# A third buffer for the gate rows and an earlier load of the output weights in the mixing stage of a hybrid decoder layer

## The chip, the cores and the metric

The kernel runs on one core of a Trainium2 chip. The metric is the device time of one execution in microseconds, as the median of several runs. The core has five engines with a queue each, worked off in order: TensorE (PE; its weight loads are shown apart as PEld), VectorE (DVE), ScalarE (ACT), GpSimd (POOL) and SyncE (SP). Here SP computes nothing, it only issues transfers between HBM and on-chip memory; POOL computes and issues some transfers too.

## The reference, cut to what matters

One decoder layer on 2048 tokens of width 1024, in float32:

```
h    = rmsnorm(x); proj = h @ w_in             # q, k, v of attention; mq, mk, mv, mo, gates of the mLSTM
o_diff  = diff_attention(q, k, v)              # 4 heads, causal, two softmaxes, p0 - lam * p1
hm      = mlstm_chunkwise(mq, mk, mv, gates)   # 4 heads, a running matrix memory C
o_mlstm = rmsnorm(hm) * sigmoid(mo)            # mo: the output gate rows
x = x + rmsnorm(concat(o_diff, o_mlstm) @ w_out)
x = x + rmsnorm(square(relu(rmsnorm(x) @ w_up)) @ w_down)
```

## The kernel before

There are four stages, and their ends overlap. The input projection (`phase_in`) writes q, k, v and the mLSTM's rows to HBM. The mixing stage (`phase_mix`) reads them back and computes both head groups. The output projection (`out_proj`) and the MLP follow. Matmuls of float32 operands that need precision use a value split in two: a rounded part and the rest. For `w_out` the ScalarE cast at line 169 makes the first part, and the GpSimd subtraction at line 170 makes the second.

The mixing stage loops over 64 units (4 heads by 16 query blocks). Each turn runs `ahead(u)`, which starts the scores of up to four units (`Q` by `K` into `s` at line 583, then row maximum, exponential at line 596 and the weighted difference of the two softmaxes at lines 604 to 606). Then come the mLSTM stages that are due, and then `values(u)`: transposes into `tp` at line 662, a ScalarE copy to `pT` at line 664, and matmuls with `V` into `pv` at line 667.

The mLSTM runs over 16 chunks of 128 tokens, with three stages each, interleaved by weight. `chunk_scores(c)` starts with the masked weights of the next chunk (`E`, lines 723 to 727). `chunk_values(c)` computes the numerators (lines 762 and 763) and, as its last step, loads chunk c+2 (`qk`, `E`, `wb`, `vaug`). `chunk_norm(c)` multiplies the gate rows `mog` on GpSimd (lines 794 and 795), stores them from there into `od` (line 796), and as its last step loads the gate rows of chunk c+2 by `chunk_gate`.

The pool `mi` holds two buffers of each of its names, `mog` too. So the gate rows of chunk c+2 go to the buffer of chunk c, and their load has to wait until the store of chunk c has landed. In every seventh turn one eighth of `w_out` is loaded into `raw` and split; the pool `raw` has two buffers.

What sets the order: a scheduler lays out each engine's instructions when the program is built. Transfers that are issued by `load`, and the one at line 167, stay among themselves in the order in which the code makes them (`keep_in_program_order`). All of them stand in SP's one queue, so a transfer that waits there holds every transfer behind it. The cast at line 169 is not kept: the scheduler may place it anywhere on ScalarE behind its load.

Of the kernel before, what the change touches and what calls it, by code (L numbers as in the profile page):

```python
# [11 lines left out]
F32 = mybir.dt.float32  # L12
F32R = mybir.dt.float32r
I32 = mybir.dt.int32
AF = mybir.ActivationFunctionType
ALU = mybir.AluOpType
# [5 lines left out]
D = 1024  # L22
# [76 lines left out]
def body(ctx: ExitStack, tc: tile.TileContext, a: dict, out: bass.AP, phases="ABCD"):  # L99
# [39 lines left out]
    with ExitStack() as mid:  # L139
        mix = phase_mix(tc, a, sc, ident, late)  # L140
        next(mix)
        for _ in first:
            pass
        raw = mid.enter_context(tc.tile_pool(name="raw", bufs=2, reuse_waits="tile"))
        wo = mid.enter_context(tc.tile_pool(name="wo", bufs=1, reuse_waits="tile"))
        w_out = [wo.tile([128, 2, D], F32R, name=f"wo{kc}") for kc in range(KC)]
        shp = mid.enter_context(tc.tile_pool(name="shp", bufs=1, reuse_waits="tile"))
        late.update(raw=raw, w_out=w_out, shp=shp)
        for _ in mix:
            pass  # L150
        hp = ctx.enter_context(ExitStack())
        hpool = hp.enter_context(tc.tile_pool(name="hp", bufs=1, side="right", reuse_waits="tile"))
        ops = {i: hpool.tile([128, 2, 4, 512], F32R, name=f"B{i}") for i in NEAR[::-1]}
        psE = hp.enter_context(tc.tile_pool(name="psE", bufs=1, side="right", reuse_waits="tile", space=PSUM))
        up = MlpUp(tc, a, sc, ops, hpool, psE)
        out_proj(tc, a, sc, ident, ops, w_out, dn, raw, shp, late["oT"], mid, up)
# [3 lines left out]
    return sc  # L160


def split(tc, raw, pool, name, src, out=None, eng=None):

    nc = tc.nc
    r = raw.tile([128, D], F32, name="raw")
    tc.keep_in_program_order(nc.sync.dma_start(r, src))
    t = pool.tile([128, 2, D], F32R, name=name) if out is None else out
    nc.scalar.copy(t[:, 0], r)
    (eng or nc.gpsimd).tensor_tensor(t[:, 1], r, t[:, 0].bitcast(F32), op=ALU.subtract)  # L170
    return t


def rsqrt_act(nc, pool, y, x, mul, add):
# [326 lines left out]
def phase_mix(tc, a, sc, ident, late):  # L501
    nc = tc.nc
    with ExitStack() as ctx:
        def pool(name, bufs, **kw):
            return ctx.enter_context(tc.tile_pool(name=name, bufs=bufs, reuse_waits="tile", **kw))
# [20 lines left out]
        def load(dst, src):  # L526

            tc.keep_in_program_order(nc.sync.dma_start(dst, src))
# [95 lines left out]
        def ahead(u):  # L624
            held = sum(1 if units[v][1] < 8 else 2 for v in pend)
            while len(pend) < 4:
                v = u + len(pend)
                if v >= len(units):
                    break
                held += 1 if units[v][1] < 8 else 2  # L630
                if held > 7:
                    break
                pend[v] = scores(v)
# [4 lines left out]
        raw, w_out = late["raw"], late["w_out"]  # L638
        mi = pool("mi", 2)
        mt = pool("mt", 1)  # L640
        cb = pool("cb", 1)
        op = pool("op", 2)
# [6 lines left out]
        def values(u, pd, rz):  # L649
            h, qb = units[u]  # L650
            load_ahead(1, u + 2)
            if qb % 4 == 0:
                outs[h] = op.tile([128, 4, 128], F32, name="o")
            o = outs[h]
            nb = qb + 1
            pv = psV.tile([128, 128], F32, name="pv")
            for j in range((nb + 3) // 4):
                m = min(4, nb - 4 * j)
                tp = psT.tile([128, 512], F32, name="tp")
                for i in range(m):  # L660
                    b = 4 * j + i
                    nc.tensor.transpose(tp[:, i * 128:(i + 1) * 128], pd[:, b * 128:(b + 1) * 128], ident)  # L662
                pT = ptp.tile([128, 512], F32, name="pT")
                nc.scalar.copy(pT[:, :m * 128], tp[:, :m * 128])  # L664
                for i in range(m):
                    b = 4 * j + i
                    nc.tensor.matmul(pv, pT[:, i * 128:(i + 1) * 128], Vs[h, j][:, i, :],  # L667
                                     start=(b == 0), stop=(b == nb - 1))
            nc.vector.tensor_scalar(o[:, qb % 4, :], pv, rz[:, 0:1], None, op0=ALU.mult)
            if qb % 4 == 3:  # L670
                head_norm(h, qb // 4, o)
# [27 lines left out]
        ms = {}  # L699
# [13 lines left out]
            ms[c] = dict(qk=qk, va=va, E=E, qw=wb)  # L713

        def chunk_gate(c):
            mog = ms[c]["mog"] = mi.tile([128, 4, 128], F32, name="mog")
            load(mog, sc["mod"][c * 128:(c + 1) * 128, :].rearrange("p (h v) -> p h v", h=4))

        def chunk_weights(c):
# [58 lines left out]
        def chunk_norm(c):  # L778
            m = ms.pop(c)
            ns, mog = m["ns"], m["mog"]  # L780
            den = ns[:, :, 128]
            rdn = s2.tile([128, 4], F32, name="rdn")
            nc.vector.scalar_tensor_tensor(rdn, den, -1.0, den, op0=ALU.mult, op1=ALU.max)
            nc.vector.tensor_tensor(rdn, rdn, gc4[:, :, c], op=ALU.max)
            nc.vector.reciprocal(rdn, rdn)
            ss = s2.tile([128, 4], F32, name="ss")
            sq = mt.tile([128, 4, 128], F32, name="sq")
            for h in range(H):
                nc.scalar.activation(sq[:, h], ns[:, h, 0:128], AF.Square, scale=rdn[:, h:h + 1],
                                     accum_out=ss[:, h:h + 1])  # L790
            rs = s2.tile([128, 4], F32, name="mrs")
            rsqrt_pool(nc, s2, rs, ss, 4, mul=1.0 / 128)
            nc.gpsimd.tensor_tensor(rs, rs, rdn, op=ALU.mult)
            nc.gpsimd.tensor_tensor(mog, mog, ns[:, :, 0:128], op=ALU.mult)
            nc.gpsimd.tensor_tensor(mog, mog, rs.unsqueeze(2).broadcast_to([128, 4, 128]), op=ALU.mult)
            nc.gpsimd.dma_start(
                sc["od"][c // 4][c % 4 * 128:c % 4 * 128 + 128, 512:1024].rearrange("p (h v) -> p h v", h=4), mog)
            if c + 2 < NT:
                chunk_gate(c + 2)

        stages = [chunk_scores, chunk_values, chunk_norm]
        for c in range(2):
            chunk_load(c)
            chunk_gate(c)
# [4 lines left out]
        for u in range(N):  # L809
            ahead(u)  # L810
            seen += units[u][1] + 2
            while stage * total < seen * 48 and stage < 48:
                stages[stage % 3](stage // 3)
                stage += 1
            if u == N - 1:
                od = raw.tile([128, D], F32, name="raw")
                late["oT"], half = gather_tile(nc, 0, sc, od, pb.tile([128, S], F32, name="p"), psT, ident, late["dn"])
                half(0)
                half(1)
            values(u, *pend.pop(u))  # L820
            if u % 7 == 6 and u // 7 < len(w_out):
                kc = u // 7
                split(tc, raw, None, None, a["w_out"][kc * 128:(kc + 1) * 128, :], out=w_out[kc])


def gather_tile(nc, tt, sc, od, p, psT, ident, dn):

    nc.sync.dma_start(od, sc["od"][tt // 4][tt % 4 * 128:tt % 4 * 128 + 128, :])
    oT = p.bitcast(F32R).rearrange("p (v k t) -> p v k t", v=2, k=KC)

    def half(b):
        tp = psT.tile([128, 512], F32, name="tp")
        for i in range(4):
            k = b * 4 + i
            nc.tensor.transpose(tp[:, i * 128:(i + 1) * 128], od[:, k * 128:(k + 1) * 128], ident)
        hi = oT[:, 0, b * 4:b * 4 + 4, :].rearrange("p k t -> p (k t)")
        lo = oT[:, 1, b * 4:b * 4 + 4, :].rearrange("p k t -> p (k t)")
        if b == 0:
            nc.scalar.activation(hi, tp, AF.Copy, scale=dn)
            nc.vector.scalar_tensor_tensor(lo, tp, dn, hi.bitcast(F32), op0=ALU.mult, op1=ALU.subtract)  # L840
        else:
            nc.scalar.copy(hi, tp)
            nc.vector.tensor_tensor(lo, tp, hi.bitcast(F32), op=ALU.subtract)

    return oT, half
# [558 lines left out]
```

## Time and profile before

| | |
|---|---|
| three runs | 2546.92, 2552.14 and 2552.46 us; median 2552.14 |
| profiled execution | 2553.45 us, of which the span from the first to the last instruction is 2551.7 us |
| mean granted TensorE clock over the span | 0.975 of full speed |
| PE busy, whole span | 2437.1 us (96%) |
| PE busy, 545 to 1085 us (mixing) | 466.25 of 540 us, at a clock of 0.91 |
| SP's waits in mixing, the largest | 219.6 us for stores of the gate rows |

All times inside the kernel are us from the start of the span. A row of the timeline gives the start, the duration, the engine, the line and operation, and in brackets how long the engine stood before it and what ended that wait. For SP a row is the issuing of a transfer; the transfer lands later.

### The profile page before, as it was taken

Reading aid. Unit: us, or ns where it says so; the run is one execution under the profiler, and the core shown is the slowest. Engines: PE = TensorE matmul, PEld = TensorE weight load, DVE = VectorE, ACT = ScalarE, POOL = GpSimd, SP = SyncE. Lnnn points to the kernel's source line nnn. Section 1 sums busy time; section 2 is a strip of 40 time slices with the busy share of each in tenths; the row PEclk is TensorE's granted clock in tenths of the full one; section 3 lists DMA queues with packets and bytes.
Section 4 is the critical chain, followed back from the end, with each engine's and each line's share of the span. In section 5 each row is a group of like instructions: output and inputs, shape, how many; then the busy total and the mean of one; then the engine's idle time right before and its main releaser. Section 6 shows DMA issues by size and latency. Waiting matters only on the chain.

```text
span 2551.7 us, 34560 instructions
## 1 busy us (share of the span) xinstructions
PE 2437.1 (96%) x12030; PEld 2040.1 (80%) x12030; DVE 1468.9 (58%) x3132; ACT 1061.1 (42%) x2103; POOL 462.0 (18%) x756
## 2 busy tenths in 40 slices
PE   8999999988889897999989999999999999999998
PEld 6888889986767686878867888888888888887886
DVE  4473431016767787647667766666665543333885
ACT  7210112325666676634434434434443332332433
POOL 0002222203645464523210000000000000000323
PEclk9999999997999998999999999999999999999999
DMA  9423432235545646335785345844458665344884
GB/s 317 134 79 91 121 111 86 58 99 120 128 96 129 130 111 144 112 120 188 240 297 197 140 148 201 335 153 165 147 177 296 228 211 172 143 156 157 297 275 142
DMA packets 288559, 424.35 MB, mean 166 GB/s; under 512 B 23584, under 2 KB 162224, under 8 KB 286848
## 3 DMA queue, kind: packets, MB, share of 16 engines
q1 hardware_dynamic: 285472, 413.55, 50.5%
q0 software_dynamic: 2912, 8.59, 1.1%
q8 instruction: 95, 1.56, 0.3%
q14 instruction: 80, 0.66, 0.1%
HBM read 283.56 MB, written 138.49 MB: 165 GB/s over the span
## 4 chain that ended last, share of the span: by engine, by line
PE 80%; DMA 9%; DVE 6%; ACT 2%; issue 1%; POOL 1%; SPq 1%; POOLq 0%; DVEq 0%; ACTq 0%
PE pd L1030 18%; PE A L1030 14%; PE B L1030 10%; PE pp L93 7%; PE pp L95 7%; PE pp L94 7%; PE s L583 4%; PE pv L667 4%; DMA br<-in_w_down_dram 3%; PE tp L662 2%; DMA Q<-Qd 1%; PE po L93 1%; PE po L95 1%; PE po L94 1%; DMA E<-Md 1%
## 5 line engine op out<-in xcount | busy, mean ns | idle before, releaser
L1030 PE MATMUL pd<-bo,ao 128*128 128x512 f32 x2688 | 615.4, 391 | 7.6 <-DVE y L1224 4.3
L1030 PEld LDWEIGHTS pd<-bo,ao 128*128 128x128 f32 x2688 | 507.2, 189 | 115.7 <-issue 4.7
L1030 PE MATMUL A<-B,w 128*128 128x512 f32 x1536 | 366.6, 394 | 10.9 <-ACT w L1130 6.7
L1030 PEld LDWEIGHTS A<-B,w 128*128 128x128 f32 x1536 | 291.3, 190 | 75.8 <-ACT w L1130 8.6
L93 PE MATMUL pp<-w,xT 128*128 128x512 f32 (+1 forms) x768 | 271.4, 359 | 8.8 <-ACT w L228 7.5
L94 PE MATMUL pp<-w,xT 128*128 128x512 f32 (+1 forms) x768 | 272.9, 355 | 0.0
L1030 PE MATMUL B<-B,w 128*128 128x512 f32 x1152 | 272.2, 389 | 0.0
L95 PE MATMUL pp<-w,xT 128*128 128x512 f32 (+1 forms) x768 | 271.2, 355 | 0.0
L1282 POOL TENSOR_TENSOR y<-y,g 128x512 f32<-128x512 f32 x32 | 48.8, 1549 | 1153.7 <-ACT jk L1276 1088.6
L1030 PEld LDWEIGHTS B<-B,w 128*128 128x128 f32 x1152 | 216.4, 188 | 45.3 <-ACT w L1130 0.3
L1249 ACT CAST ao<-ar 128x1024 fp32r<-128x1024 f32 x112 | 117.8, 1052 | 298.0 <-PE pd L1030 163.7
L1224 DVE TENSOR_TENSOR ao<-ar,ao 128x1024 fp32r<-128x1024 f32 x112 | 139.1, 1243 | 167.0 <-ACT ao L1249 166.9
L583 PE MATMUL s<-K,Q 128*128 128x512 f32 (+3 forms) x640 | 193.7, 415 | 39.6 <-DMA Q<-Qd 25.7
L1100 DVE TENSOR_TENSOR w<-wr,w 128x512 fp32r<-128x512 f32 x224 | 152.2, 688 | 123.1 <-ACT w L1130 121.8
L1130 ACT CAST w<-wr 128x512 fp32r<-128x512 f32 x224 | 136.7, 620 | 111.3 <-PE B L1030 106.4
L596 ACT ACTIVATE p<-p,nm 128x128 f32<-128x128 f32 (+15 forms) x128 | 153.7, 1201 | 45.2 <-DVE nm L595 34.3
L93 PEld LDWEIGHTS pp<-w,xT 128*128 128x128 f32 x768 | 144.4, 188 | 25.3 <-ACT w L228 8.3
L667 PE MATMUL pv<-V,pT 128*128 128x128 f32 x1088 | 155.2, 286 | 7.9 <-ACT pT L664 6.0
L667 PEld LDWEIGHTS pv<-V,pT 128*128 128x128 f32 x1088 | 144.6, 199 | 19.1 <-ACT pT L664 7.9
L583 PEld LDWEIGHTS s<-K,Q 128*128 128x128 f32 x640 | 108.3, 203 | 63.5 <-issue 19.6
L94 PEld LDWEIGHTS pp<-w,xT 128*128 128x128 f32 x768 | 144.7, 188 | 15.1 <-DVE w L229 0.3
L95 PEld LDWEIGHTS pp<-w,xT 128*128 128x128 f32 x768 | 144.6, 188 | 15.3
(260 smaller groups left out, 3621.8 us busy)
## 6 DMA issues: line engine op xcount, KB each, us to landing
ud<-u SPq DMA_DIRECT2D x224, 256.0 KB, 2.4
ar<-ud SPq DMA_DIRECT2D x112, 512.0 KB, 4.1
br<-in_w_down_dram SPq DMA_DIRECT2D x224, 256.0 KB, 3.9
wr<-in_w_up_dram SPq DMA_DIRECT2D x128, 256.0 KB, 3.3
Bd<-hl SPq DMA_DIRECT2D x40, 512.0 KB, 4.1
B<-Bd SPq DMA_DIRECT2D x10, 2048.0 KB, 13.8
Q<-Qd SPq DMA_DIRECT2D x128, 128.0 KB, 6.1
raw<-in_xT_dram SPq DMA_DIRECT2D x32, 256.0 KB, 5.2
```

The lines of the kernel that those rows point to most:

```text
L93: nc.tensor.matmul(ps, lhs[0], rhs[0], start=first, stop=False)
L94: nc.tensor.matmul(ps, lhs[0], rhs[1], start=False, stop=False)
L95: nc.tensor.matmul(ps, lhs[1], rhs[0], start=False, stop=last)
L583: nc.tensor.matmul(ps[:, :w], Q[:, var, c, qo:qo + 128], Ks[h, j][:, c, 0:w], start=(var == 0), stop=(var == 1))
L596: nc.scalar.activation(pc[:, :W], pc[:, :W], AF.Exp, bias=nm[:, c:c + 1], accum_out=Z[:, c:c + 1])
L662: nc.tensor.transpose(tp[:, i * 128:(i + 1) * 128], pd[:, b * 128:(b + 1) * 128], ident)
L667: nc.tensor.matmul(pv, pT[:, i * 128:(i + 1) * 128], Vs[h, j][:, i, :], start=(b == 0), stop=(b == nb - 1))
L1030: nc.tensor.matmul(ps, l[i], r[j], start=(first and k == 0 and m == 0), stop=(last and k == n - 1 and m == 2), skip_group_check=True)
L1100: self.nc.vector.tensor_tensor(out, x, y, op=op)
L1130: self.nc.scalar.copy(w[:, 0], src)
L1224: nc.vector.tensor_tensor(out, x, y, op=op)
L1249: nc.scalar.copy(l[:, 0], u)
```

## The change

`mog` gets three buffers, so the gate rows of chunk c+2 go to the buffer of chunk c-1. `split` is cut in two. `load_weights` issues the load of `raw` in turns 4, 11, 18 and so on, and the cast with its subtraction follows two turns later, where `split` stood before. The cast is now kept in program order with the other kept ScalarE instructions, the four exponentials of `chunk_weights`. Nothing else is added or taken away; the number of transfers and of instructions that compute is the same.

```diff
-def split(tc, raw, pool, name, src, out=None, eng=None):
+def load_weights(tc, raw, src):
     nc = tc.nc
     r = raw.tile([128, D], F32, name="raw")
     tc.keep_in_program_order(nc.sync.dma_start(r, src))
-    t = pool.tile([128, 2, D], F32R, name=name) if out is None else out
-    nc.scalar.copy(t[:, 0], r)
-    (eng or nc.gpsimd).tensor_tensor(t[:, 1], r, t[:, 0].bitcast(F32), op=ALU.subtract)
-    return t
+    def split(t):
+        tc.keep_in_program_order(nc.scalar.copy(t[:, 0], r))
+        nc.gpsimd.tensor_tensor(t[:, 1], r, t[:, 0].bitcast(F32), op=ALU.subtract)
+    return split
...
         def chunk_gate(c):
-            mog = ms[c]["mog"] = mi.tile([128, 4, 128], F32, name="mog")
+            mog = ms[c]["mog"] = mi.tile([128, 4, 128], F32, name="mog", bufs=3)
...
-            if u % 7 == 6 and u // 7 < len(w_out):
+            if u % 7 == 4 and u // 7 < len(w_out):
                 kc = u // 7
-                split(tc, raw, None, None, a["w_out"][kc * 128:(kc + 1) * 128, :], out=w_out[kc])
+                cast = load_weights(tc, raw, a["w_out"][kc * 128:(kc + 1) * 128, :])
+            elif u % 7 == 6 and u // 7 < len(w_out):
+                cast(w_out[u // 7])
```

Three places in the built programs show what moves. From line 172 on, line numbers of the changed kernel are higher by two: its line 530 is line 528 of before. In brackets stands what a row waits for: DMAHW is a transfer that SP issued earlier (it keeps at most eight open), DMASW a store that GpSimd issued, PE, DVE and Pool an engine.

SP's queue where the third chunk's gate rows, `mog` of chunk 2, and the first `raw` are loaded, before:

```order
L528 DMA vaug_4819<-mvd 128x4x128 [waits DMAHW0_49,PE_49]
L528 DMA Q<-Qd_69 64x2x256 [waits DMAHW1_49,PE_49]
...
L528 DMA Q<-Qd_69 64x2x256 [waits DMAHW4_49]
L528 DMA mog<-mod 128x512 [waits DMAHW5_49,DMASW4_49,Pool_49]
L528 DMA V<-Vd_73 128x4x128 [waits DMAHW6_49]
L167 DMA raw<-in_w_out_dram 128x1024 [waits DMAHW7_49]
```

The same place in the changed kernel:

```order
L530 DMA vaug_4819<-mvd 128x4x128 [waits DMAHW0_49,PE_49]
L167 DMA raw<-in_w_out_dram 128x1024 [waits DMAHW1_49]
L530 DMA Q<-Qd_69 64x2x256 [waits DMAHW2_49,PE_49]
...
L530 DMA Q<-Qd_69 64x2x256 [waits DMAHW5_49]
L530 DMA mog<-mod 128x512 [waits DMAHW6_49]
L530 DMA V<-Vd_73 128x4x128 [waits DMAHW7_49]
```

The load of `mog` no longer waits for a store or for GpSimd, and `raw` has moved ahead of it (of each four transfers of `Q` the first and the last stand here).

SP's queue around the third `raw` and `mog` of chunk 6, before:

```order
L528 DMA qk<-mqkd 128x4x128 [waits DMAHW2_49,Pool_49]
L528 DMA E<-Md 128x4x128 [waits DMAHW3_49,DVE_49,PE_49]
...
L528 DMA vaug_4819<-mvd 128x4x128 [waits DMAHW6_49,PE_49]
L167 DMA raw<-in_w_out_dram 128x1024 [waits DMAHW7_49]
L528 DMA Q<-Qd_69 64x2x256 [waits DMAHW0_49,PE_49]
...
L528 DMA mog<-mod 128x512 [waits DMAHW4_49,DMASW4_49,Pool_49]
L528 DMA V<-Vd_73 128x4x128 [waits DMAHW5_49]
```

And in the changed kernel:

```order
L167 DMA raw<-in_w_out_dram 128x1024 [waits DMAHW4_49]
L530 DMA K<-Kd_65 64x2x512 [waits DMAHW5_49]
L530 DMA K<-Kd_65 64x2x512 [waits DMAHW6_49]
L530 DMA Q<-Qd_69 64x2x256 [waits DMAHW7_49]
...
L530 DMA qk<-mqkd 128x4x128 [waits DMAHW3_49,Pool_49]
L530 DMA E<-Md 128x4x128 [waits DMAHW4_49,DVE_49,PE_49]
...
L530 DMA vaug_4819<-mvd 128x4x128 [waits DMAHW7_49,PE_49]
L530 DMA Q<-Qd_69 64x2x256 [waits DMAHW0_49,PE_49]
...
L530 DMA mog<-mod 128x512 [waits DMAHW4_49,DMASW1_49,Pool_49]
```

`raw` stands eleven transfers earlier, ahead of `K`, `Q` and the loads of the chunk, and `mog` of chunk 6 waits for the store of chunk 3 (DMASW1) in place of that of chunk 4 (DMASW4).

ScalarE around the third cast, before:

```order
L679 ACTIVATE oc,oss<-oc 128x128 x3
L664 COPY pT<-tp 128x384 [waits PE_49,Activation_49]
L596 ACTIVATE p,Z<-p,nm 128x768 [waits DVE_49]
L169 CAST wo_4784<-raw 128x1024 [waits DMAHW7_49]
L664 COPY pT<-tp 128x512 [waits PE_49,Activation_49]
```

And in the changed kernel:

```order
L598 ACTIVATE p,Z<-p,nm 128x768 [waits DVE_49]
L666 COPY pT<-tp 128x512 [waits PE_49,Activation_49]
L598 ACTIVATE p,Z<-p,nm 128x896 [waits DVE_49] x2
L666 COPY pT<-tp 128x128 [waits PE_49,Activation_49]
L170 CAST wo_4784<-raw 128x1024 [waits DMAHW4_49]
L598 ACTIVATE p,Z<-p,nm 128x1024 [waits DVE_49]
```

The cast stands some rows later here; the copies to `pT` that stood behind it now stand ahead of it.

## Rows read from the trace of the kernel before

**Rows 1.** Windows: length; busy us (count) of PE, PEld, DVE, ACT, POOL; clock; DMA; GB/s.

```profile
545.00:1085.00 540.00, 466.25 (x2924) 388.08 (x2923) 378.37 (x1262) 340.23 (x823) 262.95 (x589) 0.91 0.51 123
1085.00:2552.00 1467.00, 1434.62 (x6366) 1180.00 (x6364) 884.95 (x1444) 574.53 (x1019) 126.91 (x88) 0.99 0.57 199
...
605.00:1085.00 480.00, 418.61 (x2713) 349.68 (x2712) 357.40 (x1172) 323.00 (x772) 256.69 (x583) 0.94 0.49 119
```

**Rows 2.** Waits of PE, 605 to 1085: us in total, times, longest us.

```profile
PE s L583 <- DMA Q<-Qd: 21.7, 6, 8.3
PE tp L662 <- ACT pT L664: 10.1, 2, 9.9
PE s L583 <- DVE mx L590: 6.7, 5, 3.9
PE s L583 <- DVE p L587: 6.5, 10, 2.4
PE pv L667 <- ACT pT L664: 6.0, 4, 2.5
PE pv L667 <- DMA V<-Vd: 1.8, 1, 1.8
```

**Rows 3.** Waits of SP's own queue, 560 to 1110.

```profile
SPq L528 <- DMA od<-mog: 219.6, 12, 38.3
...
SPq L528 <- PE s L583: 15.6, 13, 8.2
```

**Rows 4.** Timeline of SP at three of the twelve waits for a store.

```profile
717.97 1.65 SPq L167 DMA_DIRECT2D raw<-in_w_out_dram  x1
719.70 5.15 SPq L528 DMA_DIRECT2D Q<-Qd  x4
763.24 0.34 SPq L528 DMA_DIRECT2D mog<-mod  x1
...
821.32 0.34 SPq L528 DMA_DIRECT2D mog<-mod  x1
...
832.77 5.00 SPq L528 DMA_DIRECT2D Q<-Qd  x4
...
944.32 0.34 SPq L528 DMA_DIRECT2D mog<-mod  x1
...
956.36 4.46 SPq L528 DMA_DIRECT2D Q<-Qd  x4
```

**Rows 5.** Timeline of PE where it had stood longest.

```profile
731.73 0.48 PE L662 MATMUL tp<-ident,p 128*128 128x128 f32 x1 [9.88 <-ACT pT L664]
...
843.71 1.41 PE L583 MATMUL s<-K,Q 128*128 128x512 f32 x3 [7.33 <-DMA Q<-Qd]
...
966.66 2.50 PE L583 MATMUL s<-K,Q 128*128 128x512 f32 x6 [8.26 <-DMA Q<-Qd]
```

**Rows 6.** Timeline of ACT at two of the eight casts.

```profile
730.14 1.04 ACT L169 CAST wo<-raw 128x1024 fp32r<-128x1024 f32 x1 [10.55 <-DMA raw<-in_w_out_dram]
...
803.54 1.04 ACT L169 CAST wo<-raw 128x1024 fp32r<-128x1024 f32 x1 [5.91 <-DMA raw<-in_w_out_dram]
```

**Rows 7.** Timeline of POOL: the stores of the gate rows of chunks 3 and 4.

```profile
691.56 0.60 POOL L796 DMA_DIRECT2D od<-mog  x1 [0.30 <-POOL mog L795]
...
760.38 0.55 POOL L796 DMA_DIRECT2D od<-mog  x1
```

**Rows 8.** Windows over the four longest gaps of PE behind transfers: their sum.

```profile
sum 30.00, PE 0.00 PEld 0.03 DVE 5.02 ACT 6.18 POOL 5.90; mean PE 0.00 PEld 0.01 DVE 1.26 ACT 1.54 POOL 1.47
```

**Rows 9.** Windows right behind those four gaps, columns as in the first group.

```profile
641.50:645.00 3.50, 3.46 (x12) 2.91 (x13) 1.28 (x5) 0.00 (x0) 3.50 (x5) 0.55 0.38 81
731.70:738.00 6.30, 6.27 (x27) 5.61 (x28) 3.77 (x13) 5.15 (x10) 5.40 (x13) 0.60 0.00 0
843.70:850.00 6.30, 6.29 (x25) 4.68 (x25) 1.80 (x7) 1.92 (x9) 0.61 (x1) 0.55 1.04 237
966.60:973.00 6.40, 6.34 (x28) 4.94 (x29) 2.00 (x9) 2.51 (x10) 1.39 (x1) 0.55 1.13 208
```

## The prediction, made before the changed kernel ran

> **What bounds the kernel now.** I read the windows by stage first. Behind 1085 us TensorE is busy for 1434.6 of 1467 us at a clock of 0.99; in mixing it is busy for 466 of 540 us at 0.91 [rows 1]. So the slack lies in mixing, and there TensorE, the busiest engine, is the one to follow. From 605 us on, where the first stores of the gate rows come due, it stands for 480 - 418.6 = 61.4 us [rows 1]. VectorE has 357.4 us of work in these 480, so it is near behind, and no other engine has more [rows 1].
>
> Next I read what ended TensorE's waits. The largest total is loads of `Q`, 21.7 us. Then comes a copy to `pT` on ScalarE with one wait of 9.9 us, VectorE's work on the scores with 6.7 and 6.5 us, another copy to `pT` with one wait of 2.5 us among 6.0, and a load of `V` with 1.8 us [rows 2]. The reader should ask of each what stood ahead of it. In the timeline of ScalarE the two copies stand right behind casts of `w_out` that waited 10.55 and 5.91 us for `raw` [rows 6]. So those two are late transfers as well.
>
> Then SP's own queue: 12 times it stood at a load of `mog`, waiting for a store of the gate rows, 219.6 us in total and up to 38.3 us at once [rows 3]. Its timeline shows the two together. SP finished issuing `Q` at 724.85 us and could not issue `mog` before 763.24. It was let go at 821.32, issued the `Q` of 832.77 in the burst behind it, and TensorE stood until 843.71 for that `Q`. The same happened with 944.32, 956.36 and 966.66 [rows 4, 5]. Everything that had queued behind `mog` came out at once and late. In the four longest gaps of this kind, 30.0 us together, VectorE worked for 5.0, ScalarE for 6.2 and GpSimd for 5.9 us [rows 8]. So nobody used the gaps to catch up, and they can be taken out of the time nearly whole.
>
> **The change part by part.**
>
> *The third buffer.* Each `mog` load waits for one store earlier. At 724.85 us chunk 6's load would find its store done: it now needs chunk 3's, issued at 691.56, where it needed chunk 4's, issued at 760.38 [rows 4, 7]. I don't expect the wait to go everywhere. SP also waits at the chunk's loads until TensorE has read the buffers of two chunks before, and these waits stand ahead of `mog` in the queue. But the two late `Q` need only 7.33 and 8.26 us [rows 5]. Removed on TensorE: all of the waits for `Q` and `V`, 21.7 + 1.8 = 23.5 us [rows 2].
>
> *The earlier load of `raw`.* It is issued up to eleven transfers earlier, ahead of the burst. The cast that waited 10.55 us was behind a load issued at 717.97 us [rows 4, 6], and I take the one that waited 5.91 us to be alike. With SP freed as well, `raw` should be there before the cast. Removed on TensorE: 9.9 + 2.5 = 12.4 us [rows 2]. For the other six casts I count nothing, since no wait of TensorE of that size stands behind them in its rows [rows 2].
>
> *The cast kept in place.* It is the same eight casts of 1.04 us and eight subtractions. They only stand some rows earlier or later, so the work is unchanged. It costs nothing as long as `raw` has landed. If not, all copies and exponentials behind it wait, as at 730.14 us; this cover is the slower case below.
>
> *The clock.* After each of the four gaps TensorE works at half clock for a while: the windows behind them read 0.55, 0.60, 0.55 and 0.55, a mix of the two levels of 1.2 and 2.4 GHz, and TensorE is busy for 22.4 of the 22.5 us [rows 9]. At full clock that work takes less by 3.5 x 0.45 + 6.3 x 0.40 + 6.3 x 0.45 + 6.4 x 0.45 = 1.6 + 2.5 + 2.8 + 2.9 = 9.8 us.
>
> *What the order does else.* The scheduler lays out the mixing stage anew, so that hundreds of rows of TensorE and VectorE swap places with neighbours. The trace of before can't price this. From below it gives nothing; the nearest rows are the 6.7 + 6.5 = 13.2 us that TensorE waits for VectorE's work on the scores [rows 2], which could go or double. I take a loss of one wait of the longest of these, 3.9 us [rows 2], since a stage without slack at the transfers should show more of VectorE's.
>
> *The sum.* 23.5 + 12.4 + 9.8 - 3.9 = 41.8 us. The profiled execution took 2553.45 us, 1.3 us over the median of the runs, 2552.14. From the median that is 2510.
>
> **A rule against it.** The stage's busiest engine by its share is TensorE, and the change takes no work from it; if only that work counted, the time would stay at 2552. The rows that speak against this are the 61.4 us in which TensorE stands and the half-clock stretches [rows 1, 9]. I give it 5 in 100, together with the case that transfers are hidden anyway. The Trainium skill has the rule in Perfetto Trace Analysis, section Identifying the Most-Contended Engine: optimize the engine with the highest occupancy first. The trace agrees only in part: 466 us of TensorE in 540 is the highest share, but what can be won lies on SP, which computes nothing.
>
> **The rivals.**
>
> *The block only moves (16 in 100).* SP stands at the chunk's loads or at the next store, and part of the late loads stays late. For it speaks that stores come unevenly: two that follow each other can lie 68.8 us apart, as those of 691.56 and 760.38 [rows 7], so that a single store can hold up SP even with three buffers. SP waits 15.6 us for TensorE to read `Q` already [rows 3]. Against it, the late `Q` need no more than 8.3 us. If half of the 45.7 us stays, the time is 2552 - 23 = 2529. If only the casts gain, with the clock behind 731.7 us, it is 2552 - 12.4 - 2.5 = 2537.
>
> *More than the late loads (12 in 100).* Late `E` and `qk` hold ScalarE's and VectorE's queues too, without being named in TensorE's waits. If VectorE's 13.2 us also go, the gain is 45.7 + 13.2 = 59 us and the time 2493.
>
> *Slower: the kept cast becomes a barrier (7 in 100).* The scheduler can no longer move the cast behind `raw`'s landing. If SP arrives late at `raw`, each cast costs TensorE what the worst one cost, 9.9 us of wait and 2.5 us of clock, 12.4 us [rows 2, 9]. From the saved waits on `Q` and `V`, with their clock 1.6 + 2.8 + 2.9 = 7.3, there are 30.8 us to set against it, and the two waits of before, 14.9. So it decides from (30.8 + 14.9) / 12.4 = 3.7, that is when four of the eight casts wait so long; with six the time is 2552 + 74 - 46 = 2580. Against it speaks that `raw` stands earlier in SP's queue and waits there for nothing but SP's own open transfers.
>
> **How the numbers follow.** The forecast has 60 in 100 and a range of its own from 2497 to 2524, which is the sum of 41.8 with VectorE's 13.2 us added or taken away. The rivals hold 16, 12, 7 and 5. I take the range from 2488, a little below the 2493 of the better case, to 2538, the worst part of the block that only moves; outside lie the slower case, no change, and small parts of the others, somewhat under 2 in 10. A measurement of this kernel tells about 0.2%, 5 us, from no change. Faster by more: 60 + 16 + 12 = 88; within: 5; slower: 7.
>
> **What would show it.** SP's wait at `mog` should fall from 219.6 us to well under 100. TensorE's waits for `Q` should fall from 21.7 us to under 5. No cast should wait for `raw` for more than 1 or 2 us, where two waited 10.55 and 5.91 us. The clock of the mixing stage should rise from 0.91 to about 0.94, with the stage near 500 us long in place of 540, and the stages behind it unchanged in length. The prediction is wrong if these waits go and the time stays, which would mean that VectorE's or ScalarE's chain was the limit under the gaps; or if SP stands as long as before, at `E`, `qk` or `Q` in place of `mog`.

## The result and the profile of the changed kernel

The changed kernel took 2508.52 us (median of four runs, 2505.69 to 2512.56) beside 2550.85 us for the kernel before (median of four, 2546.92 to 2552.46). The ratio is 0.9837 with a 95% interval from 0.9819 to 0.9856, so the kernel is faster by 42.3 us. The forecast was 2510 us. The profiled execution took 2512.56 us with a span of 2510.8 us and a mean granted clock of 0.983, where before had 0.975.

Windows by stage of the changed kernel. The mixing stage now ends at 1043 us. The columns are those of [rows 1].

```profile
605.00:1043.00 438.00, 409.24 (x2704) 343.15 (x2703) 354.74 (x1169) 321.40 (x764) 261.80 (x582) 0.97 0.52 125
545.00:1043.00 498.00, 456.14 (x2918) 381.08 (x2917) 375.77 (x1259) 338.66 (x815) 268.05 (x588) 0.94 0.54 130
1043.00:2511.00 1468.00, 1434.53 (x6375) 1179.55 (x6373) 885.95 (x1446) 575.98 (x1027) 128.03 (x88) 0.99 0.58 200
```

The stage is 42 us shorter, and the stages behind it kept their 1467 to 1468 us. With [rows 1], the 42 us split on TensorE in two. Its idle time fell from 540 - 466.25 = 73.75 to 498 - 456.14 = 41.86 us, by 31.9 us. Its busy time fell by 10.1 us at about the same number of matmuls, as the granted clock rose from 0.91 to 0.94.

Waits of SP's own queue in the changed kernel, 560 to 1070 us (total, times, longest):

```profile
SPq L530 <- DMA od<-mog: 54.0, 9, 17.0
SPq L530 <- PE s L585: 44.3, 22, 7.9
...
SPq L530 <- PE m L764: 33.3, 8, 6.0
SPq L530 <- DVE E L749: 28.8, 5, 9.2
...
SPq L530 <- PE pv L669: 21.6, 4, 8.2
```

The 219.6 us for stores of the gate rows [rows 3] are 54.0 now. Other waits have come up in their place: SP stands until TensorE has read `Q` (44.3 us, 15.6 before) and `V` (by `pv`), has done the matmuls into `m`, and until VectorE is done with `E`. These loads wait for a buffer that is still in use, so SP has run ahead of the engines. In sum SP stands hardly less: over all rows of this view its waits at loads (lines 167 and 528, now 530) went from 288 to 244 us, and those for anything but the stores of the gate rows from 69 to 190 us. Whether such a wait matters is not in this view. It shows only on the engine that uses the transfer.

Waits of TensorE in the changed kernel, 605 to 1043 us:

```profile
PE s L585 <- DVE p L589: 8.8, 10, 2.2
PE pv L669 <- DVE o L671: 8.7, 3, 3.5
PE s L585 <- DVE mx L592: 3.6, 7, 0.9
PE pv L669 <- ACT pT L666: 2.4, 2, 2.1
PE tp L664 <- DVE p L608: 1.8, 4, 0.7
PE tp L664 <- DVE p L844: 0.8, 1, 0.8
PE s L585 <- DMA Q<-Qd: 0.4, 1, 0.4
```

Against [rows 2], the waits for `Q` went from 21.7 to 0.4 us. Those for `V` and those before a transpose for `pT` (`tp`, 10.1 us, 9.9 of them behind a cast) are gone, and those of `pv` for `pT` went from 6.0 to 2.4. What leads now is VectorE's work: on the scores (`p`, `mx`), and on the output (`o`, which holds the buffer of `pv`).

SP's timeline of the changed kernel at the places that answer to [rows 4], and below it ScalarE's third cast, which answers to [rows 6]:

```profile
692.93 0.64 SPq L167 DMA_DIRECT2D raw<-in_w_out_dram  x1
...
704.47 3.94 SPq L530 DMA_DIRECT2D Q<-Qd  x4
710.62 0.34 SPq L530 DMA_DIRECT2D mog<-mod  x1
...
765.83 0.34 SPq L530 DMA_DIRECT2D mog<-mod  x1
...
889.31 0.34 SPq L530 DMA_DIRECT2D mog<-mod  x1
```

```profile
617.96 1.05 ACT L170 CAST wo<-raw 128x1024 fp32r<-128x1024 f32 x1
678.38 1.06 ACT L170 CAST wo<-raw 128x1024 fp32r<-128x1024 f32 x1
710.82 1.05 ACT L170 CAST wo<-raw 128x1024 fp32r<-128x1024 f32 x1
```

`mog` of chunk 6 followed its `Q` at 710.62 us, where SP had stood until 763.24. The loads of chunks 8 and 12, which had gone out at 821.32 and 944.32, went out at 765.83 and 889.31. The third `raw` was issued at 692.93, 17.9 us ahead of its cast, and no cast has a wait in brackets any more.

### The profile page after: what moved, and what is told of

Its sections match the earlier page's. It is cut to its first block, busy times and chain, and to the rows that moved or that the text cites. A ratio compares the mean times of both kernels' runs of the same rounds, so it can differ in the third digit from the quotient of the medians.

```text
span 2510.8 us, 34565 instructions
## 1 busy us (share of the span) xinstructions
PE 2426.9 (97%) x12030; PEld 2032.6 (81%) x12030; DVE 1467.3 (58%) x3132; ACT 1061.3 (42%) x2103; POOL 468.2 (19%) x756
## 4 chain that ended last, share of the span: by engine, by line
PE 80%; DVE 8%; DMA 7%; issue 2%; ACT 2%; POOL 1%; SPq 1%; POOLq 0%; DVEq 0%; ACTq 0%
PE pd L1034 16%; PE A L1034 14%; PE B L1034 10%; PE pp L93 7%; PE pp L95 7%; PE pp L94 7%; PE pv L669 4%; DMA br<-in_w_down_dram 4%; PE s L585 4%; PE tp L664 2%; PE po L93 1%; PE po L95 1%; PE po L94 1%; PE m L765 1%; DMA t<-in_x_dram 1%
## 5 line engine op out<-in xcount | busy, mean ns | idle before, releaser
L585 PE MATMUL s<-K,Q 128*128 128x512 f32 (+3 forms) x640 | 187.0, 405 | 17.3 <-DVE p L589 8.8
L589 DVE TENSOR_SCALAR_CACHE_REDUCE p<-s 128x512 f32<-128x512 f32 x192 | 129.5, 683 | 28.4 <-PE s L585 22.5
```

The lines of the kernel that those rows point to most:

```text
L585: nc.tensor.matmul(ps[:, :w], Q[:, var, c, qo:qo + 128], Ks[h, j][:, c, 0:w], start=(var == 0), stop=(var == 1))
L589: nc.vector.tensor_scalar(dst, ps[:, :w], 0.0, None, op0=ALU.add, op1=ALU.max, accum_out=mx[:, c, j:j + 1])
```

## The experiments

All that the prediction said would show it came true: SP's wait at `mog`, the waits for `Q` and of the casts, the clock and the length of the stages. But several edits were made at once. The **first theory** was that of the prediction: the third buffer frees SP's queue, and the earlier load frees the casts. **Rivals**: one of the two edits does it all; the kept cast, and not its load, frees the casts (or costs something); the remaining waits of SP still cost time. The kernel before was run anew with each of three groups of experiments, with medians of 2548.32, 2554.52 and 2553.59 us, so ratios are compared, and not times.

### One edit at a time

**The third buffer alone** (label `third_buffer_alone`).

```diff
-            mog = ms[c]["mog"] = mi.tile([128, 4, 128], F32, name="mog")
+            mog = ms[c]["mog"] = mi.tile([128, 4, 128], F32, name="mog", bufs=3)
```

> The kernel before with three buffers for the gate rows as the only edit; load and cast of the output weights as before. Theory (the wait for a store at SP's gate-row load holds back every load behind it): SP's wait for stores falls from 219.6 to about 54 us as in the changed kernel, TensorE's waits for Q from 21.7 to under 2 us, and since raw too stands behind those loads, most of the casts' waits go with it: 2508 to 2520 us. Rival (the early load of the output weights brings most of the gain): the casts still wait for raw about as long as before (32.1 us in total) and the time is 2530 to 2545 us.

Measured: 2516.62 us, ratio 0.9881 [0.9864, 0.9897], which is 31.7 us below the 2548.32 of before. SP waits 42.1 us for stores and from 605 us on TensorE does not wait for `Q`. Casts still wait, 21.0 us in all, where before had 32.1, and TensorE still waits for copies to `pT`, once for 5.3 us before a transpose. Waits of SP, then of ScalarE for `raw` before and in this kernel, then of TensorE for `pT`, then two of ScalarE's casts:

```profile
SPq L528 <- DMA od<-mog: 42.1, 8, 12.5
```

```profile
ACT wo L169 <- DMA raw<-in_w_out_dram: 32.1, 5, 11.7
```

```profile
ACT wo L169 <- DMA raw<-in_w_out_dram: 21.0, 5, 13.2
```

```profile
PE tp L662 <- ACT pT L664: 5.3, 1, 5.3
```

```profile
716.41 1.04 ACT L169 CAST wo<-raw 128x1024 fp32r<-128x1024 f32 x1 [6.03 <-DMA raw<-in_w_out_dram]
...
965.38 1.04 ACT L169 CAST wo<-raw 128x1024 fp32r<-128x1024 f32 x1 [13.25 <-DMA raw<-in_w_out_dram]
```

**The earlier load and the kept cast, without the third buffer** (label `early_load_kept_cast_alone`). This is the changed kernel with this line put back:

```diff
-            mog = ms[c]["mog"] = mi.tile([128, 4, 128], F32, name="mog", bufs=3)
+            mog = ms[c]["mog"] = mi.tile([128, 4, 128], F32, name="mog")
```

> The changed kernel with two buffers for the gate rows. Theory: SP stands at the gate rows as long as before, about 200 us in 12 waits, the late Q stay (about 20 us of TensorE's waits), only the casts no longer wait for raw; gain 12.4 us and 2.5 us of clock, 2532 to 2540 us. Rival (the early load brings most of the gain): 2508 to 2520 us.

Measured: 2536.12 us, ratio 0.996 [0.9945, 0.9975]. No cast waits for `raw`, but the late transfers are all there. Waits of SP and of TensorE in this kernel:

```profile
SPq L530 <- DMA od<-mog: 206.3, 13, 33.1
```

```profile
PE s L585 <- DMA Q<-Qd: 27.4, 5, 11.0
PE pv L669 <- DMA V<-Vd: 6.6, 2, 4.3
```

So the third buffer is the larger part: 1.2% alone, and 0.996 - 0.9837 = 1.2% again on top of the other two edits.

**The earlier load alone** (label `early_load_free_cast_alone`): two buffers, `raw` loaded two turns earlier, the cast not kept.

```diff
-        tc.keep_in_program_order(nc.scalar.copy(t[:, 0], r))
+        nc.scalar.copy(t[:, 0], r)
...
-            mog = ms[c]["mog"] = mi.tile([128, 4, 128], F32, name="mog", bufs=3)
+            mog = ms[c]["mog"] = mi.tile([128, 4, 128], F32, name="mog")
```

(The diff is against the changed kernel.)

> The kernel before with the load of the output weights two units earlier as the only edit: two buffers, cast free. Theory (the earlier load does nothing by itself, since the free cast moves up with it): casts wait 25 to 45 us for raw, SP stands about 200 us for stores, 2540 to 2565 us, the kernel before or slower. Rival (raw lands earlier in spite of it): casts wait under 10 us, 2530 to 2540 us.

Measured: 2550.6 us, ratio 0.9985 [0.9976, 0.9995]. That is less than the 0.2% that the prediction took as the least that can be told from no change. The casts still wait 22.0 us for `raw`, although it is loaded two turns earlier:

```profile
ACT wo L170 <- DMA raw<-in_w_out_dram: 22.0, 4, 9.4
```

**The kept cast alone** (label `kept_cast_alone`): before, with one line changed.

```diff
-    nc.scalar.copy(t[:, 0], r)
+    tc.keep_in_program_order(nc.scalar.copy(t[:, 0], r))
```

> The kernel before with the cast kept in program order as the only edit: two buffers, load in the turn of its cast. Theory: SP stands for the stores as before, over 200 us, raw comes late behind them, so the casts wait about as long as before, 20 to 35 us, and the late Q stay: within 8 us of the kernel before, 2540 to 2556 us. Rival (a kept cast is a barrier): the casts wait 50 us or more and the time is 2560 to 2580 us. Rival (the kept cast is itself worth the 8 us that it brought with three buffers): 2538 to 2543 us.

Measured: 2536.83 us, ratio 0.993 [0.9914, 0.9946], better than the theory or either rival had it, if by little against the last of them (2538 to 2543 us). The casts' waits fell to 11.6 us (32.1 before), but those for `Q` fell too, with SP's wait for stores hardly changed:

```profile
SPq L528 <- DMA od<-mog: 209.5, 12, 35.4
```

```profile
PE s L583 <- DMA Q<-Qd: 12.6, 5, 5.5
```

The casts' waits explain part of it. Why `Q` is waited for less is not explained by the edit itself. With the eight casts kept, the scheduler laid out the other engines anew too: 1165 of TensorE's 12030 matmuls stand at another place of the trace than before. So a place where a late `Q` is needed may have moved away from it. That is argued, not shown.

### Is it SP's queue, or the buffer?

If the queue behind a waiting `mog` is the cost, two buffers must do once `mog` is loaded from another engine's queue.

**Gate rows loaded from GpSimd, two buffers** (label `gate_rows_from_gpsimd`): before with

```diff
-            load(mog, sc["mod"][c * 128:(c + 1) * 128, :].rearrange("p (h v) -> p h v", h=4))
+            nc.gpsimd.dma_start(mog, sc["mod"][c * 128:(c + 1) * 128, :].rearrange("p (h v) -> p h v", h=4))
```

> The kernel before, two buffers, with the gate-row load issued by GpSimd in place of SP; all else as before. Theory (it is the place in SP's queue that costs, not the lateness of the gate rows): GpSimd now waits for the store, 16 waits of some 2.6 us, SP waits for no store, TensorE's waits for Q fall under 2 us; 2505 to 2525 us. Rival (the gate rows themselves come too late with two buffers and hold the norm): the time stays within 10 us of 2551.

Measured: 2524.12 us, ratio 0.9913 [0.9897, 0.9929]. The wait for the store now stands on GpSimd, where it is short, and SP has none; its waits now begin with TensorE reading `Q`. Waits of GpSimd and of SP in this kernel:

```profile
POOL mog L717 <- DMA od<-mog: 10.5, 7, 2.6
```

```profile
SPq L528 <- PE s L583: 70.2, 28, 6.4
```

TensorE's waits for `Q` are gone here too, from 605 us on. The casts still wait 28.6 us. The gain is smaller than that of the third buffer alone (0.9913 beside 0.9881), so with the cast free the two ways are not shown to be worth the same. Why is open.

**The same in the changed kernel** (label `gate_rows_from_gpsimd_early_kept`): the changed kernel with `mog` loaded from GpSimd as above, and two buffers.

```diff
-            mog = ms[c]["mog"] = mi.tile([128, 4, 128], F32, name="mog", bufs=3)
-            load(mog, sc["mod"][c * 128:(c + 1) * 128, :].rearrange("p (h v) -> p h v", h=4))
+            mog = ms[c]["mog"] = mi.tile([128, 4, 128], F32, name="mog")
+            nc.gpsimd.dma_start(mog, sc["mod"][c * 128:(c + 1) * 128, :].rearrange("p (h v) -> p h v", h=4))
```

> The changed kernel with two buffers again and the gate-row load issued by GpSimd: SP waits for no store at all, where 54.0 us of such waits are left in the changed kernel. Theory (the rest is off the path): the casts no longer wait for raw, unlike the 28.6 us with GpSimd's load alone, and the time is 2504 to 2516 us, no better than the changed kernel. Rival (the remaining 54 us still cost): 2485 to 2500 us.

Measured: 2511.57 us, ratio 0.9834 [0.9817, 0.985], no different from the change's 0.9837. With no wait for a store of the gate rows left in SP's queue, nothing more is won that could be measured. So the 54.0 us that SP still waits for them in the changed kernel lie off the path, as far as this pair can tell (each interval is some 0.2% to either side), and with an early load and a kept cast, taking the wait out of SP's queue does all that the third buffer does.

### Which edit frees the casts?

**Third buffer and kept cast, the load left where it was** (label `third_buffer_kept_cast_load_late`): before with

```diff
-    nc.scalar.copy(t[:, 0], r)
+    tc.keep_in_program_order(nc.scalar.copy(t[:, 0], r))
...
-            mog = ms[c]["mog"] = mi.tile([128, 4, 128], F32, name="mog")
+            mog = ms[c]["mog"] = mi.tile([128, 4, 128], F32, name="mog", bufs=3)
```

TensorE, VectorE, ScalarE and GpSimd have the very order of the changed kernel, instruction by instruction of the two traces. Only SP's queue differs: `raw` stands later. So this kernel shows the earlier load by itself.

> The changed kernel with the output weights loaded in the same turn as their cast, as before; three buffers, cast kept. The casts stand on the same rows of ScalarE as in the changed kernel. Theory: with SP free of the long waits raw mostly lands before the cast even so; some casts wait a few us each; 2508 to 2520 us. Rival (a kept cast becomes a barrier unless its load is early): casts wait 5 to 12 us each, 40 us or more in total, TensorE behind them, 2530 to 2560 us.

Measured: 2508.55 us, ratio 0.9845 [0.9829, 0.9862], beside 0.9837 [0.9819, 0.9856] of the change. The earlier load gives nothing that can be measured; an effect of some 0.2% would not show. ScalarE's and SP's timeline rows of the third cast, in this kernel:

```profile
713.29 1.05 ACT L169 CAST wo<-raw 128x1024 fp32r<-128x1024 f32 x1 [0.50 <-DMA raw<-in_w_out_dram]
```

```profile
703.16 0.61 SPq L167 DMA_DIRECT2D raw<-in_w_out_dram  x1
```

`raw` was issued 10.1 us ahead of its cast, and the cast waited 0.50 us. In the kernel with the third buffer alone the same load went out at 704.88 us, and ScalarE came to the free cast at 716.41 - 6.03 = 710.38, 5.5 us behind the issue, and stood until `raw` was there. For this cast a load 1.7 us earlier and a cast 2.4 us later (712.79 beside 710.38) made the difference, and `raw` was there 10 us behind its issue in place of 11.5.

**Third buffer and earlier load, the cast free** (label `third_buffer_early_load_free_cast`): the changed kernel with

```diff
-        tc.keep_in_program_order(nc.scalar.copy(t[:, 0], r))
+        nc.scalar.copy(t[:, 0], r)
```

SP's order is that of the changed kernel, row by row; all eight casts stand earlier on ScalarE.

> The changed kernel with the cast left free for the scheduler. It then stands 9 to 34 rows earlier on ScalarE than the kept cast. Theory A (the load must lie well ahead of its cast; two units are enough): no cast waits over 2 us, 2505 to 2513 us, as the changed kernel. Theory B (what counts is where the cast stands; the free cast eats up the earlier load): casts still wait 10 to 30 us in total, 2513 to 2522 us, as with the third buffer alone.

Measured: 2533.35 us, ratio 0.9917 [0.9896, 0.9938]. That is worse than the third buffer alone. The free cast follows its load forward and still stands closely behind it. ScalarE's waits for `raw`, two casts and one of their loads, and what TensorE waited for in this kernel:

```profile
ACT wo L170 <- DMA raw<-in_w_out_dram: 37.8, 7, 9.3
```

```profile
664.52 1.04 ACT L170 CAST wo<-raw 128x1024 fp32r<-128x1024 f32 x1 [8.68 <-DMA raw<-in_w_out_dram]
...
860.74 1.04 ACT L170 CAST wo<-raw 128x1024 fp32r<-128x1024 f32 x1 [9.26 <-DMA raw<-in_w_out_dram]
```

```profile
851.75 0.35 SPq L167 DMA_DIRECT2D raw<-in_w_out_dram  x1
```

```profile
PE tp L664 <- ACT pT L666: 11.9, 3, 5.1
...
PE m L764 <- DVE E L749: 5.3, 1, 5.3
```

The load of 851.75 us was there 9 us later, and ScalarE had been at the cast since 860.74 - 9.26 = 851.48. TensorE stood 11.9 us before transposes for the copies to `pT`, where the changed kernel has none of these waits. The mixing stage of this kernel:

```profile
545.00:1069.00 524.00, 469.93 (x2911) 392.06 (x2910) 368.96 (x1254) 335.80 (x813) 264.69 (x588) 0.91 0.51 123
```

Beside the changed kernel it is 26 us longer: TensorE stands 54.1 - 41.9 = 12.2 us more, and works 13.8 us longer on about the same number of matmuls, at a clock of 0.91 in place of 0.94. As its whole order was laid out anew, the run alone does not show that the casts cost all of this.

**The cast on GpSimd** (labels `third_buffer_cast_on_gpsimd`, which is before with three buffers, and `third_buffer_early_load_cast_on_gpsimd`, which is the changed kernel; neither keeps the cast):

```diff
-    nc.scalar.copy(t[:, 0], r)
+    nc.gpsimd.tensor_copy(t[:, 0], r)
```

> The kernel before with three buffers and the cast on GpSimd, load in the turn of the cast. Theory: the 8 us between the third buffer alone (2517 us) and the changed kernel (2509 us) are the 21.0 us in which casts stood on ScalarE; 2503 to 2513 us. Rival (GpSimd's queue, held by late raw, delays the weighted difference and the norms): 2515 to 2530 us.

> The changed kernel with the cast of the output weights on GpSimd in place of ScalarE, free for the scheduler. With the cast free on ScalarE this kernel took 2533 us and its casts waited 37.8 us for raw. Theory (a cast that waits on ScalarE holds the copies and exponentials behind it, and TensorE behind these): GpSimd waits instead, whose work TensorE needs later, TensorE's waits for copies to pT fall from 11.9 to under 4 us, 2505 to 2518 us. Rival (the new order of the instructions of TensorE and VectorE costs the 25 us, not the casts): 2525 to 2540 us.

Measured: 2505.96 us, ratio 0.9818 [0.9792, 0.9844], and 2517.44 us, ratio 0.9861 [0.984, 0.9881]. Waits of GpSimd for `raw` in the first and in the second:

```profile
POOL wo L169 <- DMA raw<-in_w_out_dram: 31.7, 5, 10.8
```

```profile
POOL wo L170 <- DMA raw<-in_w_out_dram: 32.1, 5, 9.6
```

A cast that waits as long as ever costs little when it waits on GpSimd, where the copies to `pT` and the exponentials are not queued behind it: in both kernels TensorE has no wait for `pT` before a transpose, where it had 5.3 and 11.9 us with the cast free on ScalarE. With the early load this takes back 0.9917 - 0.9861 = 0.0056 of the 0.0080 by which the free cast is behind the change. The first has the lowest median of all, but its interval covers the change's ratio, so it is not shown to be better. Why the second is slower than the first stays open. TensorE waits longer for the row maxima there (`mx`, 11.5 us against 5.3), and its order was laid out anew.

### Is VectorE the next limit?

**More of the weighted difference on GpSimd** (label `changed_more_on_gpsimd`): the changed kernel with

```diff
-PSH = 0.35
+PSH = 0.45
```

> The changed kernel with the share of the weighted difference that ScalarE and GpSimd take from VectorE raised from 0.35 to 0.45 of the blocks (lines 604 to 607). After the change TensorE's longest waits are for VectorE. Theory (VectorE is the next limit of the stage): VectorE's work there falls by some 10 us, TensorE's waits for it shrink, 2498 to 2506 us. Rival (GpSimd's addition, 1.35 us each, is longer than what VectorE saves and its result comes later): 2510 to 2525 us.

Measured: 2509.65 us, ratio 0.9826 [0.9811, 0.9842], no measurable difference from the change. TensorE's waits shift between VectorE's operations and do not go away. But VectorE's work on the weighted difference did not fall by the 10 us that were expected. It went from 76.4 us in the changed kernel to 75.7 here, on some 11% fewer columns. Some shapes took longer on average than in the changed kernel (896 columns: 1378 ns, 1208 there), others less (1152 columns: 1591, 1937 there); why isn't shown. So the run does not tell whether less work for VectorE would help, and the question stays open. VectorE's weighted difference (total us, mean ns) in the changed kernel and in this one, then two of TensorE's waits in this one:

```profile
L608 DVE SCALAR_TENSOR_TENSOR p<-p,cf 128x128 f32<-128x128 f32 (+7 forms) x64 | 76.4, 1195 | 0.7
```

```profile
L608 DVE SCALAR_TENSOR_TENSOR p<-p,cf 128x640 f32<-128x640 f32 (+5 forms) x64 | 75.7, 1182 | 0.9
```

```profile
PE pv L669 <- DVE o L671: 11.4, 4, 6.1
PE s L585 <- DVE p L589: 4.9, 6, 1.4
```

A fourth buffer for `mog`, or three of every tile of its pool, wasn't tried.

### The edits side by side

| ratio to before | cast free | cast kept | cast on GpSimd |
|---|---|---|---|
| two buffers, late load | 1 | 0.993 | |
| two buffers, early load | 0.9985 | 0.996 | |
| three buffers, late load | 0.9881 | 0.9845 | 0.9818 |
| three buffers, early load | 0.9917 | 0.9837 (the change) | 0.9861 |

## Why the prediction was right, point by point

The sum of 41.8 us met the 42.3 us closer than it could be expected to: the interval of the ratio is some 5 us to either side, and edits that leave the work alone moved the time by more than that. Its parts have to be judged one by one.

**What bounds the kernel: right.** Transfers behind a store that SP waited for held TensorE. Both ways of taking that wait out of SP's queue, by a buffer or by another queue, removed the waits for `Q`.

**Third buffer, 23.5 us of waits: right, and the waits for `Q` and `V` shown to go by themselves.** With the clock behind the three gaps at `Q`, 7.3 us, the prediction had 30.8 us for it; alone it gave 31.7. That close a match is partly luck, as in that kernel TensorE's waits for `pT` are shorter as well (10.1 to 5.3 us, and 6.0 to 3.0), which the prediction had put to the load. The rival that the block only moves came true on SP and not in the time: SP's other waits rose from 69 to 190 us, but TensorE waits 0.4 us for `Q`. So the prediction's sign of being wrong, that SP stands as long as before at `E`, `qk` or `Q`, was nearly met (244 us at its loads in place of 288) and meant nothing: what counts is whether an engine waits for what is behind.

**The earlier load of `raw`, 12.4 us: the size was about right, the cause wrong.** This is the step that failed. The prediction took 9.9 and 2.5 us off TensorE's waits for an earlier load. It was right to count only two casts, though five waited. The longest of the five waits ended at 970.49 us, but TensorE itself stood for `Q` until 966.66 [rows 5], and no wait of TensorE for `pT` stands behind that cast:

```profile
970.49 1.05 ACT L169 CAST wo<-raw 128x1024 fp32r<-128x1024 f32 x1 [11.68 <-DMA raw<-in_w_out_dram]
```

From the third buffer alone to the change the ratio falls by 0.9881 - 0.9837 = 0.0044, some 11 us of 2551; the prediction had 12.4 and 2.5 for the clock. But the earlier load has no part in it that could be measured: with the same order on the four computing engines it is 0.9845 without and 0.9837 with it. With two buffers and a kept cast it takes the casts' last 11.6 us of waits away, and the ratio goes from 0.993 to 0.996 all the same. With a free cast and three buffers it even stands beside a loss, 0.9881 without and 0.9917 with it. What took the waits away is the kept cast, which stands later on ScalarE than the free one beside three buffers, together with the third buffer, by which SP comes to `raw` in time. That the time between 0.9881 and 0.9845 is these waits is not shown by itself, as the kept cast also gives the other engines a new order. The prediction read that `raw` was late, and took for granted that the load was what had to move. In the kernels with a free cast the scheduler moved the cast with the load.

**The kept cast costs nothing: right for the change, wrong as a statement on the edit.** It was costed as neutral, with a slower rival in which it becomes a barrier. The opposite is so: of the kernels with the cast on ScalarE, those with a free one wait, for 21.0 to 37.8 us in all, and those with a kept one for 11.6 us or less. Alone it gave 0.7%, part of which stays unexplained. That it did not become a barrier is shown: even with the late load and three buffers its casts wait 0.5 us.

**The clock, 9.8 us: right in size.** TensorE's busy time in the stage fell by 10.1 us at about the same number of matmuls, as the clock rose from 0.91 to 0.94. That this fall lies in the four stretches that the prediction named wasn't read.

**What is given back, 3.9 us: right in size.** The waits for `Q`, `V` and `pT` that went add up to 21.3 + 1.8 + 10.1 + 3.6 = 36.8 us. Over the same stretch, from 605 us to the end of the stage, TensorE's idle time fell from 61.4 to 438 - 409.2 = 28.8 us, by 32.6. So 4.2 us came back as other waits. The largest of these is VectorE's `o`, 8.7 us, and not the work on the scores that the prediction named (13.2 us before, 8.8 + 3.6 = 12.4 now).

**Against the rule that only the busiest engine's work counts.** TensorE has the same work as before, and the time fell by 1.6%. In this stage most of what could be won lay in the queue of an engine that computes nothing, and it was found by following the waits of the busiest one.

## What to carry to other kernels

When an engine waits for a transfer, look at what stood ahead of that transfer in the queue that issued it. One load that waits for a store holds all loads behind it, and a buffer more for that one tile, or another queue for that one load, takes the wait away; then ask of each wait that remains on the issuing queue whether a computing engine waits for what is behind it. An instruction that needs a transfer should stand well behind the load in the order of its own in-order engine, or on an engine that nobody waits for; moving the load alone does not help if the instruction moves with it.

## What the runs showed of the hardware that was not expected

SP's waits of 54.0 us for stores in the changed kernel cost nothing that could be measured, while the 219.6 of before, with what went with them, were worth 31.7 us. One wait of a queue cannot be priced by its length. A load of `raw` took between 4 and 13 us from its issue until a waiting cast could go on (818.07 to 821.71 us with three buffers, an early load and a free cast; 790.12 to 803.54 in before). Waiting for `raw` cost on ScalarE (21.0 us of it at a ratio of 0.9881) and hardly on GpSimd (31.7 us at 0.9818, the same buffers and load). Some 11% fewer columns of the weighted difference for VectorE, and more for GpSimd, made VectorE's total 1% shorter (76.4 to 75.7 us). And edits that leave the work alone moved the time by 11 us (between the two kernels with the cast on GpSimd) and by up to 18 us (the kept cast alone), part of it without a wait that explains it, so a single pair of kernels is thin evidence for an effect of that size.
